# A two-block transformer layer on one core: the first merges' tiles placed over the search's, float32 element work of GpSimd on VectorE, the projections' PSUM copies on ScalarE

## The chip, the core and the metric

The kernel runs on one core of a Trainium2 chip. TensorE multiplies into PSUM; VectorE, ScalarE and GpSimd work on tiles (ScalarE and VectorE read PSUM too); SyncE issues every DMA of this kernel, in order. The metric is the time of one execution in device microseconds, as a median over runs.

## The reference

Two blocks follow each other on `x` of 2048 tokens by 1024, all float32.

```python
# first block
h = rms_norm(x, norm_g)
q, k, v, qi, ki, wi, z_a, u_b, z_b, gates = split(h @ w_in)
q, k = rope(rms_norm(q)), rope(rms_norm(k)); qi, ki = rope(qi), rope(ki)
# 128 queries at a time: index scores over all earlier keys, the 256 best are kept
iscore = einsum(relu(einsum(qi, ki)), wi); idx = top_k(where(allowed, iscore, -inf), 256)
a = softmax_over_idx(q, k) @ v * silu(z_a)
b = multiscale_pool(u_b) * silu(z_b)          # trailing means over 2, 4, 8, 16 tokens, a 128x128 map each
g = sigmoid(gates + merge_bias)
x = x + (g[0] * (a @ w_branch_a) + g[1] * (b @ w_branch_b)) @ w_out
# second block
shift, scale, gate = split(silu(c) @ w_ada + b_ada)
h = rms(x, g_pre) * (1 + scale) + shift
q, k, v, z_a, u_b, v_b, z_b, g = split(h @ w_in_2)
y_a = window_attention(rope(q), rope(k), v, sinks) * silu(z_a)   # 128 tokens back
y_b = gelu(u_b) * spatial_gate(layernorm(gelu(v_b))) * silu(z_b)
y = (sigmoid(g[0]) * (y_a @ w_proj_a) + sigmoid(g[1]) * (y_b @ w_proj_b)) @ w_out_2
x = x + gate * rms(y, g_post)
```

## The kernel before, in words

**Precision.** Every large product is made of three passes over float32r operands split into a high and a low part: high = a rounding copy on ScalarE, low = source minus high (`split`, L334 to 337). So each weight tile and each left operand costs a ScalarE cast and a subtraction. Weight tiles (`wtile`, L182) and the y of the merges are subtracted on VectorE; all other splits, those of `transposed` (L230) and of the index queries (L435), on GpSimd.

**Stages.** Tokens go in four quarters of 512 (q = 0 to 3), sixteen blocks of 128.

- `phase_a` (0 to about 300 us): for each quarter, `token_major` makes the 1064 columns of q, k, v and the index operands; their PSUM tiles are copied by `evac` (L207), which alternates between ScalarE and VectorE unless `evac_act` is set. Then norms, rotations (`rotate`, with two products on GpSimd, L362 and 363), splits, and transposes through `stacks`, whose PSUM results `evac` copies as well.
- `attention_1` (about 330 to 1556 us): units of two blocks (15 and 7 alone) in the order (8,6), (9,5), (10,4), (15), (14,0), (13,1), (12,2), (11,3), (7). Four steps overlap: the index scores of one unit (`index_scores`), the start and the end of two searches (`search`: 32 rounds that find the 256th largest score by its bits; at the end a running count of ties, masked and added to the bias, L566 to 572), and the softmax attention of a fourth (`attend`).
- `dense`, beside it: the 28 tiles of 128 columns for each quarter (z, u, gates; `uzg`, `dim_major`, matmuls on L295), in the order 3, 0, 1, 2. Their place is tied to attention: `paced` puts each group of three matmuls behind a certain attention matmul. The last four tiles of quarter 2 are left over (`self.rest`).
- First merges (to about 2040 us): `filled` makes the eight split input tiles of a quarter, `fill_1` = `heads_in` (attention output over its sums, times silu(z_a); four head groups) and `pool_in` (four groups, each with a small matmul, L843). `merge_out` multiplies them by the two branch weights (L878), weights with the gates and adds (L880, 881), splits, and runs `token_major` (L274) for the output product, which `merge_1` adds to x. `merges` makes the next quarter's inputs after four steps of a body. The modulation sums (`ada_columns`) are interleaved with the first two bodies.
- Second block: columns, post-processing (`post_2`), window attention, projections, and the second merges (2920 to 3432 us).

**Order.** The engines' instruction orders are written when the program is built: a planner goes through the instructions by priority (place in the program, raised in `urgent`), against its own timeline, and puts each on its engine when its inputs and its tile's memory are free there. An engine then runs its list in order.

**Memory.** Pools are laid out from the left or from the right of SBUF; a pool opened after another is closed takes its place, and each tile waits for the old tiles that it lies over. Before the change, the attention stage has on the left `per` (kS, vS, kI, wi), the softmax pools, `bp` (three biases) and `xp` (three score tiles and the search's scratch). After it `hp2` (the first input tiles of a merge) and `hp3` start at `per`, and `stage` follows.

## Time and profile before

| what | value |
|---|---|
| median of 3 runs | 3424.64 us (3421.09 to 3427.6) |
| the profiled execution | 3433.52 us |
| its span, first to last instruction | 3431.8 us |
| mean granted TensorE clock | 0.969 |
| TensorE busy | 3185.6 us, 93% of the span |
| VectorE busy | 2353.4 us, 69% |
| ScalarE busy | 1862.0 us, 54% |
| GpSimd busy | 820.6 us, 24% |
| HBM read and written | 467.22 and 167.38 MB |

PE is TensorE, PEld its weight loads, DVE VectorE, ACT ScalarE, POOL GpSimd, SP SyncE. A busy share over the whole span mixes stages with different limits; it is the stretches that count. The last column of a granted clock is a share of 2.4 GHz: 1.00 is the higher level, 0.50 the lower.

### The profile page before, as it was taken

The numbers are of one execution on the slowest core, as the hardware profiler recorded it, in microseconds if no ns is written. First come the engines' busy times: TensorE is split into PE (matmuls) and PEld (weight loads), VectorE is DVE, ScalarE is ACT, GpSimd is POOL, SyncE is SP. The second block draws the span as 40 slices with busy tenths as digits, with TensorE's granted clock in tenths as the row PEclk, the third lists the DMA queues.
The fourth block names the chain that finished last, engine by engine and source line by source line (L and its number), as shares of the span: only waits on it lengthen the run. The fifth ranks groups of instructions, "written<-read, shape, count | busy, mean of one in ns | idle before, by whom it ended". The sixth has DMA issues, their size and how long they took to land. (4 is left out here: it accounts for less than half of the span.)

```text
span 3431.8 us, 47878 instructions
## 1 busy us (share of the span) xinstructions
PE 3185.6 (93%) x15880; PEld 2642.8 (77%) x15880; DVE 2353.4 (69%) x4745; ACT 1862.0 (54%) x3498; POOL 820.6 (24%) x1293
## 2 busy tenths in 40 slices
PE   5997989999988999997889999999999999999998
PEld 5996767787766777875667878888888887777787
DVE  5875778889998888635887556446446455668765
ACT  3553676886666687663444333335444445764443
POOL 0432145522324365202322113102102111111100
PEclk9998999999988999998899999999999999999999
DMA  5657875435323443566886555445555446878654
GB/s 182 236 159 267 281 263 182 145 127 172 128 76 103 131 150 129 163 196 195 258 280 230 183 173 175 164 154 174 192 152 187 153 149 211 256 223 275 227 184 147
DMA packets 290824, 637.78 MB, mean 186 GB/s; under 512 B 46096, under 2 KB 100112, under 8 KB 276240
## 3 DMA queue, kind: packets, MB, share of 16 engines
q1 hardware_dynamic: 290576, 634.73, 56.7%
q8 instruction: 125, 2.05, 0.2%
q14 instruction: 123, 1.01, 0.1%
HBM read 467.22 MB, written 167.38 MB: 185 GB/s over the span
## 5 line engine op out<-in xcount | busy, mean ns | idle before, releaser
L295 PE MATMUL ps<-h,hl 128*128 128x512 f32 x5376 | 1372.9, 400 | 18.0 <-ACT st L209 16.6
L295 PEld LDWEIGHTS ps<-h,hl 128*128 128x128 f32 x5376 | 987.0, 189 | 227.0 <-ACT st L209 26.8
L274 PE MATMUL ps<-hl,h 128*128 128x512 f32 (+3 forms) x3840 | 821.5, 368 | 27.5 <-DVE st L899 9.8
L274 PEld LDWEIGHTS ps<-hl,h 128*128 128x128 f32 x3840 | 671.1, 191 | 126.2 <-DVE st L899 10.8
L337 DVE TENSOR_TENSOR hl<-raw,hl 128x1024 fp32r<-128x1024 f32 (+3 forms) x364 | 440.6, 1211 | 333.9 <-ACT hl L336 332.2
L336 ACT CAST hl<-raw 128x1024 fp32r<-128x1024 f32 (+4 forms) x380 | 366.4, 965 | 380.0 <-PE ps L274 143.2
L878 PE MATMUL ps<-h,hl 128*128 128x512 f32 x1536 | 384.4, 410 | 29.6 <-DVE g L880 9.2
L878 PEld LDWEIGHTS ps<-h,hl 128*128 128x128 f32 x1536 | 299.7, 197 | 104.9 <-ACT hl L336 11.6
L484 DVE SCALAR_TENSOR_TENSOR junk<-half,sm,junk 128x704 bf16<-128x704 int16 (+17 forms) x316 | 321.9, 1019 | 5.3
L524 POOL TENSOR_SCALAR sm<-sm 128x1 f32<-128x1 f32 x448 | 181.4, 408 | 591.6 <-DVE junk L484 297.4
L636 ACT ACTIVATE s<-s,nm 128x1024 f32<-128x1024 f32 (+7 forms) x320 | 237.7, 745 | 152.9 <-DVE nm L632 151.7
L650 PE MATMUL ps<-ident,s 128*128 128x128 f32 x1344 | 225.3, 279 | 34.1 <-ACT s L636 28.7
L655 ACT CAST th<-ps 128x512 fp32r<-128x512 f32 (+1 forms) x352 | 196.1, 572 | 84.2 <-PE ps L650 60.5
L650 PEld LDWEIGHTS ps<-ident,s 128*128 128x128 f32 x1344 | 167.0, 143 | 72.4 <-ACT s L636 42.1
L664 PE MATMUL po<-th,vS 128*128 128x256 f32 x1088 | 200.6, 290 | 4.0 <-ACT th L658 3.3
L469 DVE SCALAR_TENSOR_TENSOR score<-ps,wi,score 128x512 f32<-128x512 f32 (+3 forms) x266 | 177.6, 679 | 20.9 <-ACT ps L465 18.5
L664 PEld LDWEIGHTS po<-th,vS 128*128 128x128 f32 x1088 | 167.6, 190 | 30.0 <-ACT th L658 11.3
L526 POOL TENSOR_SCALAR sm<-sm 128x1 f32<-128x1 f32 x448 | 180.5, 403 | 40.0
L658 ACT CAST th<-ps 128x512 fp32r<-128x512 f32 (+1 forms) x288 | 156.9, 567 | 56.3 <-PE ps L657 55.1
L465 ACT ACTIVATE ps<-ps 128x512 f32<-128x512 f32 (+3 forms) x304 | 154.3, 534 | 56.1 <-PE ps L462 55.5
L483 DVE TENSOR_SCALAR junk<-half,sm 128x704 bf16<-128x704 int16 (+17 forms) x316 | 145.5, 460 | 48.0 <-POOL sm L526 43.3
L209 ACT COPY st<-ps 128x512 f32<-128x512 f32 x156 | 91.1, 584 | 135.5 <-PE ps L295 69.9
(278 smaller groups left out, 4049.3 us busy)
## 6 DMA issues: line engine op xcount, KB each, us to landing
hl<-wk SPq DMA_DIRECT2D x84, 1024.0 KB, 5.2
raw<-in_wu SPq DMA_DIRECT2D x140, 512.0 KB, 4.4
raw<-in_wd SPq DMA_DIRECT2D x128, 512.0 KB, 4.5
zd<-st SPq DMA_DIRECT2D x224, 256.0 KB, 2.9
g<-zd SPq DMA_DIRECT2D x128, 256.0 KB, 4.4
wk<-hl SPq DMA_DIRECT2D x28, 1024.0 KB, 4.8
qd<-qs SPq DMA_DIRECT2D x32, 512.0 KB, 5.7
qA<-qd SPq DMA_DIRECT2D x64, 256.0 KB, 3.4
```

Of the source, the lines that this page charges most:

```text
L274: nc.tensor.matmul(ps[b][:, :n], h[k][:, s, b * P:(b + 1) * P], wt[:, r, kk, :], start=(k == 0 and i == 0), stop=(k == KT - 1 and i == 2))
L295: nc.tensor.matmul(ps, wt[:, r, k, :], h[k][:, s, :], start=(k == 0 and i == 0), stop=(k == KT - 1 and i == 2))
L336: self.nc.scalar.copy(hi, src)
L337: (eng or self.nc.gpsimd).tensor_sub(lo, src, hi.bitcast(F32))
L484: self.nc.vector.scalar_tensor_tensor(junk, x[:, h:], thr, junk, op0=op, op1=ALU.add, accum_out=out)
L524: nc.gpsimd.tensor_scalar(one(u, e), one(p, e), one(q, e), 0.5 if bit else 1.0, op0=ALU.is_ge, op1=ALU.subtract)
L526: nc.gpsimd.tensor_scalar(one(c, e), one(u, e), w, one(c, e), op0=ALU.mult, op1=ALU.add)
L636: nc.scalar.activation(p, p, AF.Exp, scale=-1.0, bias=nm[:, h:h + 1], accum_out=x["sums"][:, c, h:h + 1])
L650: nc.tensor.matmul(pt[:, kk, e, :], ss[e][c][:, off:off + P], self.ident.bitcast(F32), is_transpose=True, start=(kk == e == 0), stop=(kk = ...
L655: nc.scalar.copy(hi, ptf)
L664: last = nc.tensor.matmul(po[:, :256], x["vap"](kt, g), th[:, r, kk], start=(kt == 0 and r == 0), stop=(kt == nkt - 1 and r == 1))
L878: nc.tensor.matmul(ps, wt[:, r, 4 * e + k, :], ab[4 * e + k][:, s, :], start=(k == 0 and i == 0), stop=(k == 3 and i == 2))
```

## The change

Three things are changed together. First, memory and order of the first merges: the search's scratch (`xp`) and biases go to the right of SBUF, the score tiles into a pool of their own on the left behind kI and wi, `hp3` and `hp2` swap places (so that hp3 lies over kS and vS, and hp2 over kI, wi and the scores), `stage` goes to the right over the search's scratch, the gates get a pool of their own; the first fill is now that of quarter 3, it stands ahead of the left-over tiles, and the merges go 3, 0, 2, 1. Second, every float32 subtraction, product and addition of whole tiles that GpSimd made goes to VectorE, and so do the two 16-bit ones at the end of the search; GpSimd keeps the search's one-column steps (L524, 526), its affine selects and one small addition of sums (L678). Third, `evac_act` is set ahead of `phase_a`, so that ScalarE makes all its PSUM copies through `evac`. Besides, qI and the search's junk tile get two buffers each.

```diff
@@ wtile, split, transposed, rotate
-        self.split(hl[:, 0, :w], hl[:, 1, :w], raw, self.weng)
+        self.split(hl[:, 0, :w], hl[:, 1, :w], raw)
-        (eng or self.nc.gpsimd).tensor_sub(lo, src, hi.bitcast(F32))
+        self.nc.vector.tensor_sub(lo, src, hi.bitcast(F32))
-                nc.gpsimd.tensor_sub(t[:, 1], f, t[:, 0].bitcast(F32))
+                nc.vector.tensor_sub(t[:, 1], f, t[:, 0].bitcast(F32))
-        nc.gpsimd.tensor_mul(B[:, :, 0, :], t[:, :, 1, :], ss[:, 0, :].unsqueeze(1).to_broadcast([P, heads, half]))
-        nc.gpsimd.tensor_mul(B[:, :, 1, :], t[:, :, 0, :], ss[:, 1, :].unsqueeze(1).to_broadcast([P, heads, half]))
+        nc.vector.tensor_mul(B[:, :, 0, :], t[:, :, 1, :], ss[:, 0, :].unsqueeze(1).to_broadcast([P, heads, half]))
+        nc.vector.tensor_mul(B[:, :, 1, :], t[:, :, 0, :], ss[:, 1, :].unsqueeze(1).to_broadcast([P, heads, half]))
@@ phase_a, index_scores, count, search, make, merge_out, post_2
-                    nc.gpsimd.tensor_sub(si[:, :, 1, :], qi, si[:, :, 0, :].bitcast(F32))
+                    nc.vector.tensor_sub(si[:, :, 1, :], qi, si[:, :, 0, :].bitcast(F32))
-            qI = self.xp.tile([P, 4, P], F32R, name="qI")
+            qI = self.xp.tile([P, 4, P], F32R, name="qI", bufs=2)
-        junk = self.xp.tile([P, S // 2], BF16, name="junk")[:, :h]
+        junk = self.xp.tile([P, S // 2], BF16, name="junk", bufs=2)[:, :h]
-            nc.gpsimd.tensor_mul(pre, pre, eq)
+            nc.vector.tensor_mul(pre, pre, eq)
-            nc.gpsimd.tensor_add(bias, bias, eq)
+            nc.vector.tensor_add(bias, bias, eq)
-            x = self.xp.tile([P, S], F32, name="score", bufs=3)
+            x = self.xs.tile([P, S], F32, name="score")
-                g = self.stage.tile([P, 512], F32, name="g", bufs=4)
+                g = self.gates.tile([P, 512], F32, name="g")
-            nc.gpsimd.tensor_mul(v, v, lng)
+            nc.vector.tensor_mul(v, v, lng)
@@ run
-            self.kI = per.tile([P, S], F32R, name="kI")
-            self.wi = per.tile([P, NB, 8], F32, name="wi")
+            idx = self.pl(es, "idx")
+            self.kI = idx.tile([P, S], F32R, name="kI")
+            self.wi = idx.tile([P, NB, 8], F32, name="wi")
...
+                self.evac_act = True
                 h3 = self.phase_a()
...
+            self.xs = self.pl(es, "xs", 3)
+            self.xp = self.pl(es, "xp", side=R)
+            self.bp = self.pl(es, "bp", self.BP, side=R)
             self.att_pools(es, 1024, self.PP, self.TP)
-            self.bp = self.pl(es, "bp", self.BP)
-            self.xp = self.pl(es, "xp")
...
-            self.evac_act = True
...
-        hp2, hp3 = self.pl(e2, "hp2", 8), self.pl(e2, "hp3", 8)
+        hp3, hp2 = self.pl(e2, "hp3", 8), self.pl(e2, "hp2", 8)
...
-            self.stage = self.pl(ep, "stage", 8)
+            self.stage = self.pl(ep, "stage", 8, side=R)
+            self.gates = self.pl(ep, "gates", 4, side=R)
             ex = self.pl(ep, "whx", 2)
             self.wpools((whl, 3), (ex, 2))
+            ab = self.filled(self.fill_1, 3)
             for _ in self.rest:
                 pass
-            ab = self.filled(self.fill_1, 0)
-            m1 = self.merges(self.fill_1, self.merge_1, 4, ab, (0, 3, 2, 1))
+            m1 = self.merges(self.fill_1, self.merge_1, 4, ab, (3, 0, 2, 1))
...
         self.stage = self.pl(e2, "stage2", 6, side=R)
+        self.gates = self.pl(e2, "gates2", 4, side=R)
```

## Rows read from the trace of the kernel before

**Rows 1.** The page, busy time by engine: us, share of span, instructions.

```profile
PE 3185.6 (93%) x15880; PEld 2642.8 (77%) x15880; DVE 2353.4 (69%) x4745; ACT 1862.0 (54%) x3498; POOL 820.6 (24%) x1293
```

**Rows 2.** Windows: stretch, length, busy us (count) by engine, PEclk, DMA share, GB/s.

```profile
core 0: us, PE busy (x) PEld busy (x) DVE busy (x) ACT busy (x) POOL busy (x), PEclk, DMA share, GB/s
250.00:300.00 50.00, 33.64 (x191) 28.68 (x190) 33.64 (x81) 22.34 (x45) 22.75 (x34) 0.76 0.62 224
900.00:1250.00 350.00, 308.07 (x1592) 251.67 (x1591) 311.79 (x695) 240.29 (x509) 135.02 (x265) 0.91 0.36 118
1450.00:1558.00 108.00, 102.26 (x577) 85.89 (x575) 32.12 (x79) 66.36 (x134) 1.40 (x2) 1.00 0.61 189
1580.00:1736.00 156.00, 120.37 (x443) 90.72 (x442) 132.47 (x204) 65.41 (x98) 44.88 (x31) 0.84 0.75 241
1736.00:1846.00 110.00, 98.52 (x404) 77.21 (x404) 93.17 (x141) 48.62 (x72) 25.91 (x16) 0.95 0.84 281
1846.00:1946.00 100.00, 95.72 (x406) 76.83 (x405) 57.27 (x68) 38.24 (x54) 15.19 (x12) 0.97 0.57 179
1946.00:2040.00 94.00, 93.17 (x413) 75.33 (x412) 53.34 (x65) 32.55 (x43) 14.62 (x11) 1.00 0.54 174
2040.00:2900.00 860.00, 847.01 (x4356) 714.23 (x4357) 450.92 (x821) 370.35 (x682) 143.78 (x121) 0.99 0.53 169
2900.00:3260.00 360.00, 332.62 (x1490) 267.41 (x1490) 250.31 (x450) 211.16 (x342) 48.22 (x32) 0.98 0.77 249
```

**Rows 3.** Windows, one body of the second merges, columns as in rows 2.

```profile
3243.00:3332.00 89.00, 89.00 (x388) 72.61 (x387) 54.22 (x106) 36.05 (x56) 0.00 (x0) 1.00 0.57 191
```

**Rows 4.** Timeline of PE, 1556 to 1592: start, us, line, count, [idle before <-releaser].

```profile
1558.06 22.70 PE L295 MATMUL ps<-h,hl 128*128 128x512 f32 x96 [0.68 <-ACT st L209]
1588.41 2.15 PE L843 MATMUL ps<-hl 128*128 128x512 f32 x3 [7.65 <-ACT hl L336]
```

**Rows 5.** Lines L572 and L664: ns min/median/max, first and last start in us.

```profile
L572 POOL TENSOR_TENSOR half<-half,eq x14: 917/2550/4051, 550.8 to 1449.1; 128x1152 bf16<-128x1152 bf16 x1, 128x896 bf16<-128x896 bf16 x1, 128x1280 bf16<-128x1280 bf16 x1, 128x768 bf16<-128x768 bf16 x1
L664 PE MATMUL po<-th,vS x1088: 274/281/416, 572.2 to 1555.7; 128*128 128x256 f32 x182
```

**Rows 6.** VectorE's groups, 3260 to 3432 us: busy, mean ns | idle before.

```profile
L337 DVE TENSOR_TENSOR hl<-raw,hl 128x1024 fp32r<-128x1024 f32 x27 | 33.0, 1223 | 42.4 <-ACT hl L336 42.3
L880 DVE TENSOR_TENSOR g<-g,ps 128x512 f32<-128x512 f32 x28 | 19.1, 683 | 7.0 <-PE ps L878 4.3 <-ACT g L871 2.6
L337 DVE TENSOR_TENSOR h<-g,h 128x512 fp32r<-128x512 f32 x14 | 9.7, 691 | 6.5 <-ACT h L336 6.3
```

**Rows 7.** VectorE's group L538 in 300 to 1450 us; line L915.

```profile
L538 DVE TENSOR_TENSOR half<-half,low 128x2048 int16<-128x2048 int16 x6 | 7.3, 1219 | 0.1
...
L915 DVE SCALAR_TENSOR_TENSOR as<-aw,cc,as x42: 735/750/1784, 1462.2 to 1796.9; 128x512 f32<-128x512 f32 x42
```

**Rows 8.** GpSimd's groups by shape: busy, mean ns | idle before.

```profile
L337 POOL TENSOR_TENSOR h<-z,h 128x512 fp32r<-128x512 f32 x32 | 47.7, 1492 | 173.3 <-ACT h L336 171.3 <-DMA rv<-rd 2.0
...
L569 POOL TENSOR_TENSOR low<-low,eq 128x2048 f16<-128x2048 f16 x1 | 5.0, 4992 | 4.9 <-DVE low L568 4.9
```

**Rows 9.** Timeline, 1570 to 1587 us, one instruction each of VectorE and GpSimd.

```profile
1571.62 1.75 DVE L803 TENSOR_TENSOR z<-z,rv 128x512 f32<-128x512 f32 x1
...
1571.53 1.29 POOL L337 TENSOR_TENSOR h<-z,h 128x512 fp32r<-128x512 f32 x1 [2.48 <-ACT h L336]
```

**Rows 10.** VectorE's groups by shape, 1600 to 1890 us.

```profile
L337 DVE TENSOR_TENSOR hl<-raw,hl 128x1024 fp32r<-128x1024 f32 x38 | 52.5, 1380 | 7.9 <-ACT hl L336 7.9
...
L337 DVE TENSOR_TENSOR h<-g,h 128x512 fp32r<-128x512 f32 x21 | 17.4, 829 | 11.4 <-ACT h L336 11.4
```

**Rows 11.** Waits: of VectorE for GpSimd; of SyncE's queue: total us, times, longest.

```profile
DVE eq L571 <- POOL low L569: 12.3, 9, 3.1
...
SPq L289 <- PE ps L295: 202.7, 25, 28.9
```

**Rows 12.** Windows of line L211 alone (VectorE's PSUM copies).

```profile
0.00:300.00 300.00, 31.98 (x62) 0.95 0.59 197
```

**Rows 13.** ScalarE's groups, 2920 to 3110 us.

```profile
L636 ACT ACT_TABLE_LOAD x16 | 20.5, 1283 | 0.7 <-DVE nm L632 0.4
```

More of the change, by code (lines that the diff above doesn't have):

```diff
@@ L331, in uzg, with split @@
         yield from self.dim_major(h, w, order, evac, kept, first)
-    def split(self, hi, lo, src, eng=None):
+    def split(self, hi, lo, src):
         self.nc.scalar.copy(hi, src)
-        (eng or self.nc.gpsimd).tensor_sub(lo, src, hi.bitcast(F32))
+        self.nc.vector.tensor_sub(lo, src, hi.bitcast(F32))
     def stacks(self, st, n, dst_tile, ps_tag):
@@ L882, in merge_out @@
             y = self.hx.tile([P, 2, 512], F32R, name="h")
-            self.split(y[:, 0], y[:, 1], gt[0], nc.vector)
+            self.split(y[:, 0], y[:, 1], gt[0])
             ys.append(y)
@@ L1132, in run @@
         ctx, R = self.ctx, "right"
-        self.weng = nc.vector
         whl = self.pl(ctx, "whl", 3)
```

## The prediction

> **What bounds the kernel now.** I read the page first. TensorE is busy for 3185.6 us of the 3431.8 us span [rows 1], so only its idle time and the time it runs at the lower clock can be won, and the question for each edit is in which stretch it gives TensorE something to do. The windows by stage come next [rows 2]. In one body of the second merges, 3243 to 3332 us, nothing holds TensorE: 89 us of 89, 388 matmuls, clock 1.00 [rows 3]. That is the yardstick for a merge body (192 matmuls into the gates, 192 of the output product): about 88.5 us. The four bodies of the first merges take 156 (the gap ahead of the first included), 110, 100 and 94 us, 460 together [rows 2], against 4 x 88.5 = 354 plus some 14 us for the 48 pool matmuls and the small ones: 92 us lost, the largest loss of any stage. The reader is to see in these rows that VectorE is busy for 132 of 156 and 93 of 110 us there and TensorE's granted clock is down to means of 0.84 and 0.95 (1.00 is 2.4 GHz, the lower level 1.2); in the fourth body VectorE has 53 of 94 and TensorE loses almost nothing. So this stage is set by VectorE and by what feeds it.
>
> Ahead of it, the timeline of TensorE shows the four left-over projection tiles (96 matmuls, 22.70 us from 1558.06), and then a gap of 7.65 us before the first matmul of the pool branch [rows 4]: the inputs of the first body are only being made. They could have been made earlier by data: the last instruction of the search starts at 1449.1 and the last attention matmul at 1555.7 [rows 5], and in the 108 us between VectorE is busy for 32 us [rows 2]. What stops it is memory: the body's tiles lie over tiles that attention still reads.
>
> Other losses are smaller: 16 us of idle at 250 to 300 us (end of the first projections, clock 0.76), 42 us at 900 to 1250 (VectorE busy 312 of 350, clock 0.91), 27 us at 2900 to 3260 [rows 2].
>
> **The change, part by part.**
>
> *Merges' tiles over the search's, quarter 3 first.* The score tiles and kI now lie where the first eight input tiles of a merge go, the search's scratch where the stage tiles go. Both are free when the search is over, about 1450, and quarter 3's attention blocks (12 to 15) come before the last two units, so fill_1(3) can run beside the last softmaxes instead of after them. Its cost on VectorE, with 0.69 us for a 128x512 instruction when GpSimd is idle [rows 6]: five for each of four head groups (13.8 us); in the pool branch per group silu, difference, scaling and two splits (five at 0.69, 0.2 for the small split) and ten adds over all: 14.6 + 6.9 = 21.5 us. Together 35 us, which fit into the 76 us that VectorE has free there.
>
> VectorE's demand per body, GpSimd idle: 16 weight splits of 1.22, 16 gate products and 8 output adds of 0.68, 8 sums and 8 splits of 0.69 [rows 6]: 19.6 + 16.4 + 11.0 = 47 us. The modulation columns add 48 instructions of 0.75 [rows 7] = 36 us over the first two bodies. So afterwards: first body 47 + 35 (next fill) + 18 = 100, less some 10 us that VectorE can do ahead while TensorE works off the left-over tiles: 90; second 100; third 47 + 35 = 82, so TensorE sets it (91 with the pool matmuls); fourth 90. Sum 371, and 385 if the first two run VectorE at 93%. Before it was 460 behind the left-over tiles: a gain of 75. DMA takes 10 of this back as I judge it: it ran at a share of 0.75 to 0.84 and 241 to 281 GB/s in the two first bodies [rows 2], and the same bytes less one fill have to come in less time. I take -65. Bounds: -25 (only the gap of 8 us and half of one fill's 35), and -92 (all the loss).
>
> *GpSimd's float32 products and splits to VectorE.* A split of 128x512 takes 1.49 us on GpSimd [rows 8] and 0.69 on VectorE [rows 6]. It isn't 0.69 more for VectorE, though: while GpSimd runs one, a VectorE instruction with two SBUF inputs stretches. The timeline shows L803 at 1.75 us from 1571.62, beside a GpSimd split that begins at 1571.53 [rows 9], against 0.69. By groups, a 128x1024 weight split takes 1.380 in 1600 to 1890 and 1.223 in the last 172 us where GpSimd does nothing, the split of g 0.829 against 0.691 [rows 6, 10]. The four fills hold 64 such GpSimd instructions: 48 x 0.69 + 16 x 0.2 = 36 us that VectorE takes up, against up to 1.06 us each (1.75 - 0.69) of stretching that goes; at half of it, 34. So the two cancel in the merges. The demand above already holds the moved work and no stretching, so nothing is added here; had nothing been released, the 35 us would lie inside the bound of -25.
>
> In the search there are 14 masks (L569) and 14 adds (L572), 384 to 2048 elements wide; on GpSimd the widest takes 4.99 us [rows 8]. The nearest VectorE row is a two-byte TENSOR_TENSOR of 2048: 1.219 us [rows 7]. 17,024 elements twice at that rate is about 20 us. Away go 12.3 us in which VectorE waits for L569 [rows 11], and stretching, at most GpSimd's whole time for them, 83 us at 2.44 ns an element; I take a third, 27, as most of the instructions beside them read PSUM or one tensor. Net about -19 us of VectorE work over the search, somewhat under half of it on the path: -8. Bounds -20 and +10 (no release, all on the path where VectorE is at 89%).
>
> In the second block 160 GpSimd instructions go the same way: 96 of 512 elements (66 us on VectorE at 0.69), 32 of 320 (about 15) and 32 of 128 (6). Against these 87 us stand, by the same half of 1.06 us, some 70 of stretching over the 128 larger ones. VectorE is busy for 451 of 860 us and 250 of 360 there [rows 2], and TensorE, at 847 of 860, covers it in the first part. If that cover were gone the 17 us would show. I take -5, from 2900 to 3260 us, where a fill's splits come 0.8 us sooner each (bounds -15 and +8).
>
> *Projections' PSUM copies on ScalarE.* VectorE gives up 62 copies, 32 us, in the first 300 us [rows 12] and takes the rotations and splits of that stage, some 39 us by the rates above; without the stretching it ends with less. ScalarE gets about 28 us more. TensorE is full there until the end at 250 to 300 us, where transposes, copies, casts and splits of the last blocks alternate over two banks. I take -4; bounds -12 (the faster splits shorten that chain), +8 (ScalarE has casts and copies in one queue and becomes that chain's limit).
>
> *The price at the end of attention.* The fill puts 8 sigmoids among exponentials. Beside the second attention 16 table loads for the exponential alone took 1.283 us each [rows 13]. So up to 16 loads, 20.5 us, plus about 13 us of sigmoids and casts, come on top of 66 us in 108 [rows 2]: 100 of 108. It fits, but exponentials get later, and the projection tiles are tied to attention's progress. I take +8, bounds 0 and +25.
>
> The Trainium skill (ScalarE: Activation LUTs, What ACT_TABLE_LOAD costs) gives 2.66 us for a switch, the load and as much again of draining. By it the fill would add 43 + 13 us and ScalarE would need 122 of 108 us, 14 us of delay; the rows show no idle time of that size ahead of the loads (0.7 us for all 16).
>
> *Two buffers for qI, the separate gate pool, the order of hp2 and hp3.* qI's second buffer takes away waits for its load; as VectorE paces that stretch I count nothing beyond the -8. The gate pool has the same size as before. Quarter 0, which the second block begins with, is now second of four and still done some 180 us before its use.
>
> Sum: -65 - 8 - 5 - 4 + 8 = -74. The profiled execution took 3433.52 us (span 3431.8 and 1.7 around it); 3433.5 - 74 = 3359. The median of the runs shown is 8.9 us lower, 3424.64: I predict 3351.
>
> **The rivals.** (1) *The fill pays half its gain back*: ScalarE or DMA becomes the bound. For it: 100 of 108 us of ScalarE, DMA at a share of 0.84. Against: the projection tiles give TensorE other work. (By the price of a switch on the Trainium skill's page above, it would be the likelier of the two.) Merges -45, end of attention +25, the rest 0: 3405; with half of the rest's -17, 3396. (2) *The planner leaves the fill behind attention*, since it comes after all attention and projections in program order. Then the 7.65 us gap and a VectorE-bound first body stay; what is left is the missing stretching, about -25: 3400. Against: the modulation sums, which also come later in the program, do start at 1462 us now [rows 7], as soon as there is memory. (3) *More than summed*: all 92 us of the merges, 20 of the search, 12 of the first stage, the other two terms as above: 3304. (4) *Slower*: SyncE's queue is served in order. If the order written out has the fill's loads ahead of projection weights, and the search's tiles come free later than planned, SyncE stands and TensorE runs dry. Three weight slots cover about 16 us (24 matmuls, 5.5 us each); to eat up the gain of 74 SyncE would have to stand for some 90 us. Its longest wait for a matmul is 28.9 us [rows 11]. At 100 us: 3435. (5) *No change*: memory elsewhere still holds the fill and VectorE's added work cancels the missing stretching.
>
> **How the numbers follow.** The sum as forecast (3320 to 3385): 0.58. Rivals 1 and 2 (3385 to 3415): 0.20 together. Rival 3: 0.10. Rival 4: 0.08. Rival 5: 0.04. About 0.2% (7 us) is what a measurement of this kernel can tell from no change: faster 0.88, same 0.04, slower 0.08. The range of 3300 to 3405 holds the first case, rival 3 and most of rivals 1 and 2, and leaves out about 2 in 10.
>
> **What would show it.** Right: sigmoids and head sums (L168, L801) from about 1455 us, no gap between the left-over tiles and the first body, bodies of about 92, 100, 93 and 90 us at a clock near 1.00, GpSimd busy only with the search's bits, no 128x512 VectorE instruction near 1.75 us. Wrong: attention ending over 15 us later, first bodies over 110 us with VectorE under 85% (then DMA), or a search stretch longer than now. What would break the prediction most is a different order of the instructions in the whole attention stage.

## The result, and the profile after

The changed kernel takes 3367.07 us, median of four runs (3363.71 to 3370.96), against 3422.86 us for the kernel before in the same job: ratio 0.9831, 95% interval 0.9814 to 0.9849. So it is faster, by 56 us, inside the forecast's range and 16 us above the time it named. The profiled span goes from 3431.8 to 3366.8 us.

The page of the changed kernel, busy time by engine, against [rows 1]:

```profile
PE 3165.3 (94%) x15880; PEld 2633.6 (78%) x15880; DVE 2326.4 (69%) x5055; ACT 1904.2 (57%) x3578; POOL 368.8 (11%) x913
```

TensorE does the same 15,880 matmuls in 20 us less. GpSimd has lost more than half of its work, and VectorE, which carries 310 instructions more, is busy for 27 us less. The windows of the changed kernel, by the same stages as [rows 2], columns as there:

```profile
250.00:300.00 50.00, 42.04 (x244) 34.91 (x243) 29.61 (x102) 33.32 (x71) 0.00 (x0) 0.93 0.90 316
900.00:1250.00 350.00, 318.93 (x1657) 258.74 (x1656) 300.14 (x708) 254.40 (x541) 117.96 (x291) 0.94 0.37 121
1405.00:1539.00 134.00, 125.48 (x693) 104.24 (x692) 48.75 (x113) 99.59 (x184) 0.20 (x1) 0.99 0.51 160
1574.00:1689.00 115.00, 102.75 (x420) 79.61 (x419) 105.47 (x198) 49.86 (x73) 0.00 (x0) 0.94 0.89 293
1689.00:1796.00 107.00, 99.47 (x411) 77.77 (x412) 93.84 (x148) 44.87 (x66) 1.97 (x3) 0.97 0.87 280
1796.00:1895.00 99.00, 94.64 (x408) 76.32 (x407) 64.30 (x100) 42.45 (x63) 0.00 (x0) 0.98 0.65 208
1895.00:1987.00 92.00, 91.65 (x408) 74.46 (x407) 53.70 (x71) 32.53 (x43) 0.00 (x0) 1.00 0.52 168
```

The first body went from 156 to 115 us; at 115 and 107 us the first two still stand well above the 92 of the fourth, with VectorE at 105 of 115 and 94 of 107 and DMA at a share of 0.89 and 0.87. The timeline of TensorE around the left-over tiles shows what [rows 4] didn't have:

```profile
1539.03 1.56 PE L295 MATMUL ps<-h,hl 128*128 128x512 f32 x6
1540.42 2.23 PE L843 MATMUL ps<-hl 128*128 128x512 f32 x9
1547.54 9.76 PE L295 MATMUL ps<-h,hl 128*128 128x512 f32 x29 [4.90 <-DMA hl<-wk]
1557.14 0.86 PE L843 MATMUL ps<-hl 128*128 128x512 f32 x3
1557.83 15.83 PE L295 MATMUL ps<-h,hl 128*128 128x512 f32 x67
```

The gap ahead of the first body is gone, as forecast, but a new one of 4.90 us stands ahead of the left-over tiles: the pooling's matmuls (L843) come first, and the tiles' weights (wk) are loaded only then.

The stages of the profiled executions are compared in the table below, in us: from the start to the first projection matmul (L295), to the end of attention's last matmul (L664), to the end of the last left-over tile, to the end of the fourth first-merge body, to the end of the program. The kernels e1 to e12 are those of the experiments behind it. Each row is one execution, and two that have a stage in the same order differ in it by 3 to 5 us: 283.9 and 287.2 in the first stage with the old copies and splits, 271.2 to 275.5 with the new ones, 1265.4 to 1269.6 in attention for the changed kernel, e6, e8, e10 and e11.

| kernel | first stage | attention | left-over tiles | four bodies | second block | span |
|---|---|---|---|---|---|---|
| before | 287.2 | 1268.8 | 24.8 | 457.2 | 1393.8 | 3431.8 |
| after | 271.3 | 1267.9 | 34.5 | 412.7 | 1380.4 | 3366.8 |
| e1_memory | 283.9 | 1284.2 | 34.5 | 412.6 | 1392.9 | 3408.1 |
| e2_vector | 280.5 | 1252.5 | 24.8 | 442.2 | 1376.3 | 3376.3 |
| e3_copies | 282.2 | 1269.9 | 24.7 | 455.6 | 1392.6 | 3425.0 |
| e4_no_memory | 275.5 | 1253.3 | 24.8 | 443.5 | 1380.2 | 3377.3 |
| e5_beside | 273.6 | 1294.8 | 38.6 | 451.9 | 1412.1 | 3471.0 |
| e6_fill_last | 271.2 | 1269.6 | 24.7 | 434.5 | 1375.6 | 3375.6 |
| e7_no_sigmoid | 272.7 | 1264.9 | 33.9 | 415.1 | 1373.0 | 3359.6 |
| e8_heads_first | 272.9 | 1265.4 | 24.8 | 434.4 | 1378.1 | 3375.6 |
| e9_one_buffer | 273.7 | 1246.4 | 51.0 | 414.7 | 1373.5 | 3359.3 |
| e10_own_slots | 274.8 | 1266.0 | 27.9 | 437.4 | 1378.5 | 3384.6 |
| e11_ada_spread | 272.6 | 1269.6 | 33.0 | 415.5 | 1374.8 | 3365.4 |
| e12_three | 273.3 | 1248.6 | 24.7 | 445.0 | 1375.3 | 3366.9 |

The spans differ by 65 us where the medians differ by 56, as the profiled execution of the kernel before (3433.5 us) lies 11 us above its median. Of the 65 us, 16 come from the first stage, 44.5 from the bodies and 13 from the second block; the left-over tiles give 10 back, and attention stands where it stood. This even attention turned out to be two large effects of opposite sign.

### The profile page after: what moved, and what is told of

It reads as the page before. It is cut to its first block, busy times and chain, and to the rows that moved or that the text cites. A ratio compares the mean times of both kernels' runs of the same rounds, so it can differ in the third digit from the quotient of the medians.

```text
span 3366.8 us, 47635 instructions
## 1 busy us (share of the span) xinstructions
PE 3165.3 (94%) x15880; PEld 2633.6 (78%) x15880; DVE 2326.4 (69%) x5055; ACT 1904.2 (57%) x3578; POOL 368.8 (11%) x913
## 4 chain that ended last, share of the span: by engine, by line
PE 65%; DVE 10%; DMA 9%; ACT 6%; issue 5%; POOL 4%; SPq 1%; DVEq 0%; ACTq 0%; POOLq 0%
PE ps L295 28%; PE ps L274 18%; PE ps L878 5%; PE po L664 3%; PE ps L628 3%; PE ps L650 3%; POOL sm L524 2%; POOL sm L526 2%; DMA z<-zd 1%; DMA g<-zd 1%; ACT junka L489 1%; PE ps L657 1%; DVE junk L484 1%; DVE hl L337 1%; PE ps L462 1%
## 5 line engine op out<-in xcount | busy, mean ns | idle before, releaser
L295 PE MATMUL ps<-h,hl 128*128 128x512 f32 x5376 | 1383.9, 401 | 29.3 <-ACT st L209 21.9
L295 PEld LDWEIGHTS ps<-h,hl 128*128 128x128 f32 x5376 | 990.7, 190 | 238.8 <-ACT st L209 31.9
L337 DVE TENSOR_TENSOR hl<-raw,hl 128x1024 fp32r<-128x1024 f32 (+4 forms) x380 | 424.7, 1118 | 334.9 <-ACT hl L336 325.1
L636 ACT ACTIVATE s<-s,nm 128x1024 f32<-128x1024 f32 (+7 forms) x320 | 237.8, 745 | 129.9 <-DVE nm L632 128.6
L484 DVE SCALAR_TENSOR_TENSOR junk<-half,sm,junk 128x704 bf16<-128x704 int16 (+17 forms) x316 | 309.7, 995 | 1.6
L524 POOL TENSOR_SCALAR sm<-sm 128x1 f32<-128x1 f32 x448 | 202.1, 455 | 945.1 <-ACT junka L489 567.6
L650 PE MATMUL ps<-ident,s 128*128 128x128 f32 x1344 | 234.5, 285 | 28.2 <-ACT s L636 20.9
L664 PE MATMUL po<-th,vS 128*128 128x256 f32 x1088 | 202.8, 291 | 13.1 <-ACT th L658 9.6
L664 PEld LDWEIGHTS po<-th,vS 128*128 128x128 f32 x1088 | 167.3, 190 | 43.1 <-ACT th L658 21.2
L483 DVE TENSOR_SCALAR junk<-half,sm 128x704 bf16<-128x704 int16 (+17 forms) x316 | 125.0, 412 | 63.9 <-POOL sm L526 63.4
```

What stands on the lines that cost most here:

```text
L295: nc.tensor.matmul(ps, wt[:, r, k, :], h[k][:, s, :], start=(k == 0 and i == 0), stop=(k == KT - 1 and i == 2))
L337: self.nc.vector.tensor_sub(lo, src, hi.bitcast(F32))
L484: self.nc.vector.scalar_tensor_tensor(junk, x[:, h:], thr, junk, op0=op, op1=ALU.add, accum_out=out)
L524: nc.gpsimd.tensor_scalar(one(u, e), one(p, e), one(q, e), 0.5 if bit else 1.0, op0=ALU.is_ge, op1=ALU.subtract)
L636: nc.scalar.activation(p, p, AF.Exp, scale=-1.0, bias=nm[:, h:h + 1], accum_out=x["sums"][:, c, h:h + 1])
L650: nc.tensor.matmul(pt[:, kk, e, :], ss[e][c][:, off:off + P], self.ident.bitcast(F32), is_transpose=True, start=(kk == e == 0), stop=(kk = ...
```

## The experiments

**One part of the change at a time.** Four kernels, each the kernel before with some parts of the change, 3 rounds each in one job (before: 3427.77 us).

e1_memory: the places and order of the tiles and the fill and the second buffers of qI and junk, nothing else (edit in short).

```
+ idx = self.pl(es, "idx")            # kI, wi
+ self.xs = self.pl(es, "xs", 3)      # scores
+ self.xp / self.bp  ... side=R       # scratch, masks; qI, junk bufs=2
+ hp3 before hp2; stage, gates side=R
+ ab = self.filled(self.fill_1, 3) ahead of self.rest; order (3, 0, 2, 1)
```

> The kernel before with the new memory layout and the new place and order of the fills alone. Prediction's theory (the fill beside the softmaxes and the shorter first bodies are the gain): 40 to 55 us faster than before, first merge body starts without a gap, first two bodies about 115 and 105 us, first stage and search as before. Rival (what VectorE loses to GpSimd's instructions is the gain, the layout only moves the fill): under 20 us faster, first two bodies together still over 240 us.

Measured: 3410.18 us, ratio 0.9950 (0.9931 to 0.9969). The bodies win 44.6 us, but attention loses 15.4 and the left-over tiles 9.7. The time is the rival's, the bodies are not: the first two took 115 and 108 us, as the prediction's theory had them, and not over 240. What that theory left out is the loss ahead of them.

e2_vector: GpSimd's products and splits on VectorE, nothing else.

```
- (eng or self.nc.gpsimd).tensor_sub(lo, src, hi.bitcast(F32))
+ self.nc.vector.tensor_sub(lo, src, hi.bitcast(F32))
  ... and the same for L230, L362, L363, L435, L569, L572, L1015
```

> The kernel before with GpSimd's products and splits on VectorE alone. Prediction's theory: the terms of search and second block, 10 to 15 us faster; the four first bodies, gap included, stay within 12 us of 460. Rival (the stretching of VectorE by GpSimd is the gain): 30 us faster or more, first bodies together under 430 us. If the 16 us that the first stage has gained come from the shorter splits and rotations, the first dense matmul starts near 275 us instead of 287.

Measured: 3381.68 us, ratio 0.9866 (0.9846 to 0.9887). This alone is most of the gain, 46 us by the medians, and the rival's time. It is spread over every stage: 7, 16, 15 and 17.5 us in first stage, attention, bodies and second block by the two profiles, whose spans differ by 55.5 us. The bodies, at 442 us, lie between the two theories. The page of e2_vector:

```profile
PE 3167.4 (94%) x15880; PEld 2635.3 (78%) x15880; DVE 2372.6 (70%) x5125; ACT 1865.6 (55%) x3500; POOL 361.6 (11%) x913
```

VectorE took over 380 instructions and its busy time rose by 19 us only. At their durations in this run (99 us for 192 splits, 92 for the rest) the moved ones are 191 us. The instructions that VectorE had before got 135 us shorter, added up by line and shape: 300 weight splits went from 1284 to 1223 ns, 16 products of 128x640 (L361) from 1430 to 815. (Neighbours overlap a little in the trace, so such sums of durations differ by more than the busy time.) The order of the instructions changed with the move too; what that has of the 46 us was not separated.

e3_copies: `self.evac_act = True` set ahead of phase_a, nothing else.

> The kernel before with all PSUM copies of the first stage on ScalarE alone. Prediction's theory: 0 to 4 us, no measurable difference, first dense matmul at 283 to 290 us. Rival (the copies are what has brought the first stage 16 us): 10 us faster or more, first dense matmul near 275 us.

Measured: 3426.96 us, ratio 0.9996 (0.9983 to 1.0009): no change, as the prediction's theory said; the rival's 10 us are not there. The first stage is 5 us shorter in the profile, little more than such stages differ by, and the interval of the ratio leaves room for 6 us at most.

e4_no_memory: the edits of e2 and e3 together, that is the change without its memory part.

> The changed kernel with the memory layout and the fills' place and order taken back. Prediction's theory: 15 to 25 us faster than before, 35 to 45 us slower than the changed kernel, the gap of about 8 us ahead of the first body back. Rival (the parts overlap, since both relieve VectorE in the first bodies): 35 us faster than before or more.

Measured: 3375.07 us, ratio 0.9848 (0.9828 to 0.9868). That is the rival's time, and the gap ahead of the first body is back. The first stage wins 12 us, where e2 has 7 and e3 5. The changed kernel's ratio lies 0.0017 below this one, 6 us, within both intervals: on top of the other parts the memory part moves stages by 10 to 31 us, but that it shortens the whole is not shown clear of the noise (10.5 us by the two profiles).

**Why VectorE's part is so large.** e5_beside: the changed kernel, with GpSimd busy again but out of every chain.

```
+ def beside(self, t, n, half=False):
+     ...
+     nc.gpsimd.tensor_copy(d[:, 0:1], t)               # one element, for the moment
+     ...                                               # in pieces of m columns:
+     nc.gpsimd.tensor_mul(d[:, :m], d[:, :m], d[:, :m])  # scratch, nothing reads it
  def split(...): ... self.nc.vector.tensor_sub(lo, src, ...)
+     self.beside(...)
```

> The changed kernel with work put back on GpSimd beside it: wherever the change took an operation from GpSimd (from the attention of the first block on, not in the first stage), VectorE keeps it and GpSimd in addition multiplies a scratch tile of nearly the same size, which nothing reads. Its output is unchanged. Theory one (VectorE was stretched while GpSimd ran, so taking GpSimd out frees VectorE): the stretch comes back on VectorE though no chain goes through GpSimd; of the 48 us that the VectorE part won behind the first stage at least 25 go, so 3392 to 3415 us. Theory two (the chains were slow because they went through GpSimd, whose operations take about twice VectorE's time): nothing reads what GpSimd does here, so at most 10 us go, 3367 to 3377 us.

Measured: 3470.83 us, ratio 1.0136 (1.0115 to 1.0157): 104 us above the changed kernel and above the kernel before too. The page of e5_beside:

```profile
PE 3182.4 (92%) x15880; PEld 2639.5 (76%) x15880; DVE 2425.3 (70%) x5055; ACT 1915.5 (55%) x3586; POOL 800.4 (23%) x1439
```

VectorE executes the same 5055 instructions as in the changed kernel, and is busy for 99 us longer because GpSimd is busy for 432 us more. The timeline of e5_beside shows single cases, first a weight split of VectorE alone, then the same split next to a scratch product of GpSimd, and another such product:

```profile
1678.22 1.22 DVE L355 TENSOR_TENSOR hl<-raw,hl 128x1024 fp32r<-128x1024 f32 x1
...
1682.68 0.99 POOL L346 TENSOR_TENSOR scr<-scr 128x480 f32<-128x480 f32 x1
1683.07 1.68 DVE L355 TENSOR_TENSOR hl<-raw,hl 128x1024 fp32r<-128x1024 f32 x1
...
1663.83 2.60 POOL L346 TENSOR_TENSOR scr<-scr 128x480 f32<-128x480 f32 x1
```

The split that begins 0.39 us into GpSimd's 0.99 us takes 0.46 us longer, and GpSimd's own product takes 2.60 us elsewhere: both engines pay. Theory two is out, and theory one's stretching is there: work on GpSimd that nothing reads costs VectorE almost a quarter of GpSimd's time. But the 104 us are no measure of what the stretching had of e2's gain. Here 99 us of it go with 104 us of time, more than theory one's upper end; in e2 135 us less of it went with 46. Two more things are in e5: the one-element copies hold their source tiles until GpSimd has come to them, and from 523 us on the planner put VectorE's instructions in another order than in the changed kernel. How much of the 104 us each is was not separated. The Trainium skill (SBUF — State Buffer, SBUF: two separate sides) says that the two engines' shared port pair is locked for a whole instruction and the second one waits. The trace agrees with a wait on either side: 1.68 against 1.22 us, a wait for most of the 0.60 us that GpSimd's product had left, and 2.60 against 0.99 us.

**What the early fill costs at the end of attention.** Three kernels, with e5 in one job (before: 3423.96 us).

e6_fill_last:

```
- ab = self.filled(self.fill_1, 3)
  for _ in self.rest: pass
+ ab = self.filled(self.fill_1, 3)
```

> The changed kernel with quarter 3's fill written after the four left-over tiles again; the memory layout and the order 3, 0, 2, 1 stay. Theory one (the layout frees the buffers and the planner then takes the fill up by itself as soon as it can; the written place only decides who goes first at the end of attention): the fill's first operations stay ahead of attention's end, the left-over tiles go back from 34.5 to about 25 us and the merges keep most of their 31 to 45 us: 3355 to 3368 us. Theory two (the written place is what brings the fill forward): the fill starts behind attention as before, the merges fall back, and the time is that of the kernel without the memory part, 3373 to 3385 us.

Measured: 3375.61 us, ratio 0.9860 (0.9838 to 0.9883). Half of each theory: the fill's head sums still start at 1412 us (1409 in the changed kernel), and up to 1522 us TensorE, VectorE and ScalarE have the same order as there, so the layout, not the written place, brings them forward; the left-over tiles go back to 24.7 us, yet the bodies lose 22.

e8_heads_first:

```
- ab = self.filled(self.fill_1, 3)
+ ab = [self.hslot() for _ in range(8)]
+ self.heads_in(3, self.od, self.rd, self.zd, ab[0:4])
  for _ in self.rest: pass
+ self.pool_in(3, ab[4:8])
```

> The changed kernel with quarter 3's fill cut in two: the heads ahead of the four left-over tiles, the pooling, which takes slots of the weights' ring and accumulator banks, behind them. Theory one (the gap of 4.9 us ahead of the left-over tiles and their slower pace come from ring slots that the pooling holds until attention gives its PSUM banks back): the left-over tiles go from 34.5 back to about 25 us, the merges lose at most 3, so 3356 to 3362 us. Theory two (the first body waits for the pooling anyway, and what the left-over tiles gain is lost again ahead of it): 3363 to 3373 us.

Measured: 3378.44 us, ratio 0.9866 (0.9840 to 0.9892). The left-over tiles run as before, and what they gain is lost again, as theory two has it, with 5 us more than its range. The timeline of e8_heads_first:

```profile
1540.38 22.70 PE L295 MATMUL ps<-h,hl 128*128 128x512 f32 x96 [0.68 <-ACT st L209]
1562.93 2.24 PE L843 MATMUL ps<-hl 128*128 128x512 f32 x9
1565.00 0.40 PE L878 MATMUL ps<-h,hl 128*128 128x512 f32 x1
1568.83 11.54 PE L878 MATMUL ps<-h,hl 128*128 128x512 f32 x42 [3.43 <-ACT h L336]
```

The pool matmuls now come behind the tiles, and the first body takes 134 us instead of 115. Tiles and bodies together are 459 us here and in e6, 447 in the changed kernel: the 4.90 us gap is a price that pays.

e10_own_slots (a later job, before: 3428.31 us) tried to have both:

```
- self.wpools((whl, 3), (ex, 2))
+ self.wpools((ex, 2))
  ab = self.filled(self.fill_1, 3)
+ self.wpools((whl, 3))
  for _ in self.rest: pass
+ self.wpools((whl, 3), (ex, 2))
```

> The changed kernel with the weights' ring cut in two around the end of attention: quarter 3's pooling takes its slots from the two new ones alone, the four left-over tiles from the three old ones alone, and from the first body on all five are one ring again. Theory one (the gap of 4.9 us ahead of the left-over tiles and their slower pace come from pooling that holds the ring until attention gives back its PSUM banks): their weights are loaded while attention still runs, the stretch from attention's end to the last left-over tile goes from 34.5 back to about 25 us, the merges lose at most 4, so 3357 to 3363 us. Theory two (the pooling's own chain, its products and splits, is what the left-over tiles and then the first body wait for): pooling with two slots comes later still, and the time is 3365 to 3378 us.

Measured: 3388.46 us, ratio 0.9888 (0.9860 to 0.9916). The left-over tiles come down to 27.9 us, so the ring was what delayed their weights. But with two slots the pooling's first nine matmuls, one piece from 1540 to 1543 us in the changed kernel, are spread from 1542 to 1551, and the bodies take 437.4; in the first, TensorE stands for 7.8 us at 1601 us until ScalarE has cast a weight tile. Theory two, and slower than forecast by it; where all of the bodies' 25 us arise was not followed up.

e7_no_sigmoid (sigmoids of quarter 3 replaced by copies, with e5 in one job):

```
- self.nc.scalar.activation(t, z, AF.Sigmoid)
+ self.nc.scalar.activation(t, z, AF.Identity if plain else AF.Sigmoid)
  ... plain: quarter 3 of the first block; the same for its gates (L871)
```

> The changed kernel with the sigmoids of the first block's quarter 3 (its fill and its gates) replaced by plain copies of the same size, so that its output leaves them out. Theory one (the early fill makes ScalarE change between the tables of sigmoid and exp while attention still runs, 11 loads of 1.28 us, and attention's chains wait for it): the loads go, attention's end comes 8 to 15 us earlier and the time is 3352 to 3361 us. Theory two (the end of attention is later because the fill's operations and loads as such stand in its queues): within 4 us of the changed kernel, 3363 to 3371 us.

Measured: 3363.08 us, ratio 0.9820 (0.9798 to 0.9841), which overlaps with the changed kernel's. TensorE's order is the same in both kernels to the end. Attention is 3 us shorter, no more than equal kernels differ by; the median is 4 us lower. Counted behind attention's 897th output matmul (of 1088), at 1394 us and ahead of the fill in the changed kernel, the difference is clearer: the rest of attention takes 137.4 us here, 144.8 in the changed kernel and 142.0 to 144.1 in e6, e8, e10 and e11. So the loads cost something. The changed kernel has eleven of them between 1405 and 1539 us (ScalarE's groups), e7 none:

```profile
L168 ACT ACT_TABLE_LOAD x5 | 6.4, 1283 | 4.5 <-DMA z<-zd 4.5
L636 ACT ACT_TABLE_LOAD x5 | 6.4, 1283 | 0.1
...
L871 ACT ACT_TABLE_LOAD x1 | 1.3, 1283 | 0.0
```

They set some 5 to 7 us of attention's end, less than theory one's 8 to 15, and the time is theory two's. The 2.66 us per switch of the Trainium skill (ScalarE: Activation LUTs, What ACT_TABLE_LOAD costs) isn't seen here either: the five loads of L636 have 0.1 us of idle time ahead of them together, and behind each of the eleven the next activation starts within 0.02 us.

e9_one_buffer (in one job with e10):

```
- qI = self.xp.tile([P, 4, P], F32R, name="qI", bufs=2)
+ qI = self.xp.tile([P, 4, P], F32R, name="qI")
- junk = self.xp.tile([P, S // 2], BF16, name="junk", bufs=2)[:, :h]
+ junk = self.xp.tile([P, S // 2], BF16, name="junk")[:, :h]
```

> The changed kernel with one buffer each, as before, for the indexer's query tile (qI) and for the count's scratch (junk); all else stays. With the memory layout, attention's stage took 1265 to 1269 us in every version, wherever the fill stood and with or without its sigmoids, and 1253 us without the layout. Theory one (the second buffers let the planner issue index products and counts earlier and so shift attention's own work back): attention's stage goes back to about 1253 us and the time to 3351 to 3358 us. Theory two (the new places of the pools, left and right, cost it): within 4 us of the changed kernel, 3363 to 3371 us.

Measured: 3366.33 us, ratio 0.9820 (0.9797 to 0.9844): the same as the changed kernel, and yet attention is 21.5 us shorter. Theory one on the stage, theory two on the time. Counted from the first projection matmul, attention's 897th output matmul (of 1088) comes at 1110.2 us, against 1123.1 in the changed kernel and 1112.6 in e4_no_memory: 13 us, all ahead of the fill, belong to the second buffers; which of the two, and by what change of order, was not separated. The rest, 8.6 us, arises behind it, where the changed kernel runs the fill. For the fill no longer comes early; its head sums (L801), first in the changed kernel and then in e9_one_buffer:

```profile
L801 DVE TENSOR_TENSOR top<-top,bot x32: 679/688/693, 1409.1 to 3155.6; 128x512 f32<-128x512 f32 x32
```

```profile
L801 DVE TENSOR_TENSOR top<-top,bot x32: 679/684/693, 1504.7 to 3148.1; 128x512 f32<-128x512 f32 x32
```

They start 96 us later. By the sizes in the code the search's scratch is 17.8 KB per partition with the second buffers and 13.8 without, and the stage tiles over it take 16.5: without them the stage tiles reach into the masks (bp), which attention reads to its end. That is read from the code; no run tests it. And the left-over tiles take 51.0 us instead of 34.5: the pooling's matmuls are spread among them from 1527 to 1570 us, and they wait for their weights, in the timeline of e9_one_buffer:

```profile
1549.76 7.18 PE L295 MATMUL ps<-h,hl 128*128 128x512 f32 x24 [5.31 <-DMA hl<-wk]
1556.78 0.86 PE L843 MATMUL ps<-hl 128*128 128x512 f32 x3
1563.13 6.84 PE L295 MATMUL ps<-h,hl 128*128 128x512 f32 x22 [5.50 <-DMA hl<-wk]
```

**Two attempts at a better version**, 5 rounds each (before: 3426.00 us).

e11_ada_spread:

```
- self.merge([(self.some(m1, 32), 164.0), (self.ada_columns(), 120.0)])
- for _ in self.some(m1, 24): pass
+ self.merge([(self.some(m1, 48), 246.0), (self.ada_columns(), 120.0)])
+ for _ in self.some(m1, 8): pass
```

> The changed kernel with one number moved: the sums for the second block's columns (ada_columns) are spread over the first three bodies of the first merges, not over two; nothing is left out. Theory one (the first two bodies are long, 115 and 107 us against 92 for the fourth, because VectorE and the transfers carry the fill and these sums at once there): the four bodies together go from 413 to 393 to 405 us, and the time to 3350 to 3360 us. Theory two (the fill's own chain and its transfers alone set the first bodies): the third body gains what the first two lose, and the time stays within 4 us of the changed kernel, 3363 to 3371 us.

Measured: 3367.16 us, ratio 0.9831 (0.9816 to 0.9847), no change. The edit hardly did what it says, so it decides nothing about the bodies. Line L915 in the changed kernel and in e11_ada_spread, 1540 to 2000 us:

```profile
L915 DVE SCALAR_TENSOR_TENSOR as<-aw,cc,as x42: 731/745/754, 1563.1 to 1754.2; 128x512 f32<-128x512 f32 x42
```

```profile
L915 DVE SCALAR_TENSOR_TENSOR as<-aw,cc,as x42: 734/746/754, 1564.6 to 1789.3; 128x512 f32<-128x512 f32 x42
```

The sums end 35 us later, still inside the second body.

e12_three: e9's single buffers, e6's order and e11's spread in one kernel.

> The changed kernel with three edits: one buffer each for qI and junk, quarter 3's fill written behind the left-over tiles, and the sums for the second block's columns spread over three bodies; nothing is left out. Theory one (each cost found in the runs goes with its edit): first stage 272, attention 1246 to 1253, left-over tiles 25, merges 424 to 434 and the rest as in the changed kernel 1380, so 3345 to 3360 us, below the changed kernel. Theory two (with one buffer the planner puts the fill off until attention's last 15 us, and what attention gains comes back in the first body): 3362 to 3375 us.

Measured: 3373.37 us, ratio 0.9850 (0.9832 to 0.9868). Attention has its 1248.6 us and the left-over tiles their 24.7, and the first body takes 152 us, nearly as in the kernel before (155). Theory two. No version beat the changed kernel beyond the measurement. Not run: single buffers with the scratch padded to its larger size, which by the reading above would keep the early fill and drop the 13 us.

## Why the prediction was right in sum

The direction, the stage with the largest gain (the bodies) and the range held. But two terms were wrong by some 35 to 40 us each, in opposite directions: by the runs that hold one part each, the memory part gives 18 us where the prediction has 57 (-65 and +8), and the other parts 53 where it has 17 (e1, e4). That these add up to 71 us, near the 74 forecast, is luck. Together they gave 56 and not 71, since both shorten the same bodies: 44.6 us by the one, 13.7 by the other, 44.5 by both. That overlap is about what the forecast is off by, 16 us.

**Merges, -65: too large.** The fill does run beside the last softmaxes, the gap of 7.65 us is gone, and fills and bodies follow as described. The bodies win 44.6 us with the memory part alone and 30.8 on top of the other parts. Bodies of 92, 100, 93 and 90 us were named as the sign, 375 together; the sum itself holds 395, with the first two at about 97 and 107 us and 10 for DMA. 115, 107, 99 and 92 came. The step that failed is the first body's. VectorE's work was counted well for the four together, 90, 100, 82 and 47 us against 105, 94, 64 and 54 measured, but with one fill, that is four head groups, in each of the first three. The planner put seven head groups into the first (VectorE's groups of the changed kernel, 1574 to 1689 us):

```profile
L804 DVE TENSOR_TENSOR z<-z,top 128x512 f32<-128x512 f32 x7 | 4.8, 683 | 0.0
```

So VectorE has 15 us more to do there than forecast, and at a share of 92% the body takes 18 us more than the sum has for it. What the transfers, at shares of 0.89 and 0.87 in the first two bodies, have in it was not separated.

**End of attention, +8: at its upper bound.** Measured +24.3 on top of the other parts (attention 14.6, left-over tiles 9.7) and +25.1 alone. The reason given, sigmoids among exponentials, is a small part: e7 takes them away and wins 5 to 7 us of attention's end. Two mechanisms that the prediction set at nothing make up the most of it. The second buffers of qI and junk cost 10 to 13 us of attention ahead of the fill (e4 and e9 against the changed kernel); the prediction put qI's at nothing or a gain, and junk's does not stand in it. And the pooling holds the weights' ring ahead of the left-over tiles, 9.7 us (e6, e8, e10). Rival 1 had the end of attention at +25 and the merges at -45. It was right in both numbers for the memory part, and missed in time only because the other parts gave more. Its reason, ScalarE or DMA as the bound, is not shown: ScalarE's loads have 5 to 7 us in it, and DMA's part stays open.

**GpSimd's work to VectorE, -13 with the search: the step that failed most.** The loads were about right: 182 us of moved work forecast, 191 measured; 131 us of stretching released, forecast without the first stage, 135 measured with it. What failed was "the two cancel": the balance of VectorE's busy time was taken for the balance of the path. With VectorE's busy time up by 19 us, the time fell by 46. Why is in part argued. An operation on GpSimd is late by its own duration (a split of 512 elements 1.49 us there [rows 8], 0.68 on VectorE now) and makes the VectorE instruction next to it late, and either can stand in a chain at whose end TensorE waits. By the waits in the trace of the kernel before, TensorE stood directly behind the moved operations for only 3.3 us, VectorE for 31 and ScalarE for 12. e5 shows that such work costs time even where nothing reads it, but neither share of the 46 us was measured alone. No instruction of L803 is near 1.75 us any more [rows 9], as forecast:

```profile
L803 DVE TENSOR_TENSOR z<-z,rv x32: 623/688/694, 1413.8 to 3162.2; 128x512 f32<-128x512 f32 x32
```

**Masks of the search.** The rate taken from a two-byte row of 1.219 us for 2048 elements was right; the changed kernel has 1.208 and 1.207 us at the widest (lines L569 and L572):

```profile
L569 DVE TENSOR_TENSOR low<-low,eq x14: 354/784/1208, 519.9 to 1403.0; 128x1152 f16<-128x1152 f16 x1, 128x896 f16<-128x896 f16 x1, 128x1280 f16<-128x1280 f16 x1, 128x768 f16<-128x768 f16 x1
L572 DVE TENSOR_TENSOR half<-half,eq x14: 360/788/1207, 521.6 to 1404.7; 128x1152 bf16<-128x1152 bf16 x1, 128x896 bf16<-128x896 bf16 x1, 128x1280 bf16<-128x1280 bf16 x1, 128x768 bf16<-128x768 bf16 x1
```

The last of them starts 44 us earlier than in [rows 5]. In e2, attention's stage is 16 us shorter, twice the 8 forecast.

**First stage, -4: 8 to 16 us**, from 283.9 and 287.2 us in the two kernels with the old stage to 271.2 to 275.5 with the new one: around the bound of -12. Copies on ScalarE and splits on VectorE shorten one chain, as the bound had it, and each alone gives less than both (282.2 and 280.5 us): 250 to 300 us went from 33.6 to 42.0 us of TensorE, at a clock of 0.93 after 0.76.

**Second block, -5: 13.4 us with all parts, 17.5 in e2**, near and beyond its bound of -15. It comes from GpSimd's part, as e1 and e3, without it, stay within 1.2 us of the kernel before; that the step is the same as in the merges is argued.

**The rivals.** Rival 3 had all 92 us of the bodies; 44.5 came. Of 2, 4 and 5 nothing is left: the fill starts at 1409 us, 4 us behind the search; SyncE's longest wait for a projection matmul is 20.7 us against 28.9 [rows 11]; and GpSimd's part alone decides the sign.

## What to carry to other kernels

Count an elementwise operation on GpSimd by the chain it stands in and by what it does to VectorE beside it, not by the busy time that it spares VectorE: here VectorE was busy for 69% of the span before and after, and 46 us were won by the move. Work that is brought forward into a stage takes from that stage: with the memory part alone, tiles and bodies of the merges won 35 us and attention gave 15 of them back, so the stages on both sides belong into one sum, and so does each buffer that only makes the room for it. Where a planner orders the instructions, an edit in the written order may move little (e11), or nothing until 17 us before a stage's end (e6), and an edit of buffers may move much (e9): look up the first start of the moved lines before reading the time.

## What the runs showed of the hardware

The loss beside GpSimd is mutual and large in sum: 432 us more of GpSimd's work, none of it read, lengthened the same 5055 VectorE instructions by 99 us, and single GpSimd products of 480 elements took 0.99 or 2.60 us. The other way round, 380 operations less on GpSimd made the instructions that VectorE already had 135 us shorter. The activation table loads took 1283 ns in each group, and of the eleven between 1405 and 1539 us each had its next activation start within 0.02 us behind it. These eleven, 14 us of loading with the engine busy for 100 of 134 us, cost attention's end 5 to 7 us when they were compared with none.
